# Weight sums kept within the SSD half, and transposes emitted one weight tile later

## The chip, the cores and the metric

The kernel runs on one core of a Trainium2 chip. The core has a matrix engine (TensorE, PE in the profile, with its weight loads shown as PEld), a vector engine (VectorE, DVE), a scalar engine (ScalarE, ACT), GpSimd (POOL) and a queue engine (SyncE, SP). Each takes its instructions in order. SP and POOL issue the transfers here. The metric is device time in microseconds; the median of three runs of the kernel before is 900.42 us (898.77 to 902.17).

## What is computed

Two layers over a sequence of 512 tokens and 1024 channels, in float32: a bidirectional SSD mixer, then a bidirectional gated linear attention (GLA), each with a residual, and a norm at the end. Cut to what matters:

```
def ssd_mixer(u, ...):
    z, xbc, dt = jnp.split(u @ w_in, [D_INNER, D_INNER + SSD_CONV_DIM], axis=-1)
    xbc = jax.nn.silu(dwconv(xbc, conv_w, conv_b)).astype(f32)
    xh, bm, cm = jnp.split(xbc, ...)
    y = (ssd_scan(xh, dt[:, :, 0], a[0], bm, cm)
         + rev(ssd_scan(rev(xh), rev(dt[:, :, 1]), a[1], rev(bm), rev(cm)))
         + xh * d_skip.astype(f32)[:, None])
    y = y.reshape(bsz, seq, D_INNER) * jax.nn.silu(z.astype(f32))
    y = rmsnorm(y.reshape(bsz, seq, SSD_GROUPS, ...), gnorm.reshape(SSD_GROUPS, -1))
    return y.reshape(bsz, seq, D_INNER).astype(u.dtype) @ w_out

def gla_mixer(u, ...):
    q, k, v, z, gl = jnp.split(u @ w_in, ...)
    ...
    o = gla_scan(q, k, v, lg[:, :, 0]) + rev(gla_scan(rev(q), rev(k), rev(v), rev(lg[:, :, 1])))
    o = rmsnorm(o, onorm).reshape(bsz, seq, D_INNER) * jax.nn.silu(z.astype(f32))
    return o.astype(u.dtype) @ w_out
...
h = h + ssd_mixer(rmsnorm(h, ssd_norm[0]), ...)
h = h + gla_mixer(rmsnorm(h, gla_norm[0]), ...)
return rmsnorm(h, final_norm)
```

## The kernel before

**Matmuls and weight tiles.** Every large product is made of three passes (`mm3`, lines 149 to 151): both operands are split into a high part `whi`, `uh` and a rest `wlo`, `ul`, and the product of the two rests is left out. The weights come through one list of tiles of 512 KB (`Weights`). A tile is loaded by SP into one of three `wraw` buffers (line 68), split by ScalarE (line 88 or 93) and VectorE (line 89 or 94), and used by 24 matmuls of 512 columns (12 in the block products of the GLA half). `W.next()` hands out the tile at place `W.pos`; it first emits the splits up to two tiles ahead and then calls whatever stands in `W.beside` for this place. The SSD half has the tiles 0 to 64, counted from 0; the GLA half begins with tile 65.

**The SSD half.** Eight groups g. For each, `proj_group` computes B, C and two tiles of x (matmuls `pch`), with a convolution on VectorE (line 530) and a tanh on ScalarE (line 534); every second group begins with four tiles for z (`ptk`). The scan of group g - 1 (`scan_group`, a generator) is emitted in steps between the tiles of group g. Its steps: transposes of x and B (`ptx` line 590, `ptb` line 595), copied out by ScalarE (`xt`, `bt`); the product `cb`; the decay weights of four chunks (`weights`: ScalarE lines 653 and 661, VectorE lines 658 and 662) on `bct`; the states (`pts`); then for each half of the sequence `outputs` (matmuls `pti` lines 677 and 679, `pyi` line 694, VectorE lines 700 to 704, squares on ScalarE line 708, the root on GpSimd lines 317 and 318, scaling on ScalarE line 711, giving `y`) and `transposed` (four transposes `pty` line 719, split into `yh`, `yl`, which the output projection `po` reads). `bct` is a broadcast of 1 MB, one for each group and half, loaded by SP (line 575) into three buffers, so the load for a half waits until the `pyi` of three halves earlier have read theirs. The last output projection (`pr`) and the second norm (`ptn`) end the half.

**The GLA half.** Four heads. v and z of a head come from seven block products (`pb`) in place of eight, and these need four sums of weight blocks, `w1` to `w4`, of 1 MB each. They are made in DRAM by transfers that GpSimd issues (`Blocks.step`, eight to a head, 32 in all: a copy at line 274, or an accumulating transfer at line 272), in the list of the program named `wsumw`. Each is paced: `add_manual_dep` makes it wait for the last split emitted so far. After the block products come the scores (`bd` line 1010, `pta` lines 1018 and 1019), the output projection of the head before (`po`), q and k of the next, and the outputs (`pto`, `ptyg`).

**What sets the order.** A scheduler orders each engine's instructions by priority, beginning from the order in which the code emits them. `tc.high_priority(offset=-100)` puts the transposes of `trans` 100 places behind. The places of the sums are a table of tile numbers:

```
n1 = last1 + 1
at = [8 + (n1 - 10) * i // 26 for i in range(26)] + [n1 + i for i in (20, 26, 32, 37, 42, 47)]
```

## Time and profile before

| | us |
|---|---|
| median of three runs | 900.42 (898.77 to 902.17) |
| profiled execution | 896.58 |
| its span, first to last instruction | 894.9 |
| TensorE busy | 845.0 |
| VectorE busy | 680.5 |
| ScalarE busy | 510.7 |
| GpSimd busy | 95.6 |

The rows that follow below are from this one profiled execution. Times are in microseconds from the start of the span. Matmuls overlap each other, so TensorE's busy share is not its share of peak; what counts is where it stands still and for whom. A row of the timeline gives start, duration, engine, line, operation, output<-inputs, shapes, how many instructions are merged, and in brackets the idle time of the engine before it with the engine that ended it.

### The profile page before, as it was taken

The numbers are of one execution on the slowest core, as the hardware profiler recorded it, in microseconds if no ns is written. First come the engines' busy times: TensorE is split into PE (matmuls) and PEld (weight loads), VectorE is DVE, ScalarE is ACT, GpSimd is POOL, SyncE is SP. The second block draws the span as 40 slices with busy tenths as digits, with TensorE's granted clock in tenths as the row PEclk, the third lists the DMA queues.
The fourth block names the chain that finished last, engine by engine and source line by source line (L and its number), as shares of the span: only waits on it lengthen the run. The fifth ranks groups of instructions, "written<-read, shape, count | busy, mean of one in ns | idle before, by whom it ended". The sixth has DMA issues, their size and how long they took to land.

```text
span 894.9 us, 11286 instructions
## 1 busy us (share of the span) xinstructions
PE 845.0 (94%) x3976; PEld 688.2 (77%) x3976; DVE 680.5 (76%) x1044; ACT 510.7 (57%) x1078; POOL 95.6 (11%) x156
## 2 busy tenths in 40 slices
PE   7999999999999999998799999989999989999996
PEld 5778778788888788887677777868787878778875
DVE  5499889897678986779696799877946785588644
ACT  5338698746575466654665466674527542665333
POOL 3001011101011001010102510020002000110012
PEclk9999999999999999999999999999999999999999
DMA  6447578555867575864350236428643763245202
GB/s 227 120 133 273 142 190 228 157 155 190 165 184 216 131 246 118 225 167 127 108 197 24 65 110 203 120 49 215 207 118 73 216 190 87 71 151 179 71 1 94
DMA packets 90198, 132.92 MB, mean 149 GB/s; under 512 B 7969, under 2 KB 49149, under 8 KB 87966
## 3 DMA queue, kind: packets, MB, share of 16 engines
q1 hardware_dynamic: 78716, 97.46, 34.6%
q0 software_dynamic: 11424, 34.74, 17.2%
q8 instruction: 31, 0.51, 0.2%
q14 instruction: 25, 0.20, 0.1%
q10 hardware_dynamic: 2, 0.00, 0.0%
HBM read 129.96 MB, written 35.78 MB: 185 GB/s over the span
## 4 chain that ended last, share of the span: by engine, by line
PE 60%; DVE 14%; DMA 9%; ACT 8%; issue 5%; POOL 3%; POOLq 0%; SPq 0%; ACTq 0%; DVEq 0%
DMA bct<-cumd 5%; PE pch L150 5%; PE pch L149 5%; PE pch L151 4%; PE po L150 4%; PE po L151 4%; PE po L149 4%; PE pb L149 3%; PE pb L151 3%; PE pb L150 3%; PE pyi L694 3%; PE ptk L149 3%; PE ptk L151 3%; PE ptk L150 3%; DVE wlo L89 2%
## 5 line engine op out<-in xcount | busy, mean ns | idle before, releaser
L89 DVE TENSOR_TENSOR wlo<-wraw,whi 128x1024 fp32r<-128x1024 f32 (+1 forms) x114 | 140.4, 1234 | 76.8 <-ACT whi L88 76.1
L88 ACT CAST whi<-wraw 128x1024 fp32r<-128x1024 f32 (+1 forms) x114 | 118.9, 1043 | 137.1 <-PE pch L150 40.6
L150 PE MATMUL pch<-ul,whi 128*128 128x512 f32 (+2 forms) x336 | 133.4, 397 | 0.0
L151 PE MATMUL pch<-uh,wlo 128*128 128x512 f32 (+2 forms) x336 | 132.7, 395 | 0.6 <-DVE wlo L89 0.5
L149 PE MATMUL pch<-uh,whi 128*128 128x512 f32 (+2 forms) x336 | 132.9, 396 | 0.0
L151 PEld LDWEIGHTS pch<-uh,wlo 128*128 128x128 f32 (+2 forms) x336 | 62.5, 186 | 15.0 <-DVE wlo L89 1.5
L149 PEld LDWEIGHTS pch<-uh,whi 128*128 128x128 f32 (+2 forms) x336 | 62.5, 186 | 13.8
L150 PEld LDWEIGHTS pch<-ul,whi 128*128 128x128 f32 (+2 forms) x336 | 62.5, 186 | 13.7 <-issue 0.3
L530 DVE SCALAR_TENSOR_TENSOR cv<-pch,colA,cv 128x511 f32<-128x511 f32 (+1 forms) x96 | 70.9, 743 | 0.7
L93 ACT ACTIVATE whi<-wraw,colB 128x512 fp32r<-128x512 f32 x58 | 38.8, 716 | 37.7 <-PE pch L150 17.3
L653 ACT ACTIVATE bct<-bct,eb 128x128 f32<-128x128 f32 x128 | 41.4, 391 | 22.2 <-DMA bct<-cumd 22.2
L149 PE MATMUL ptk<-whi,uh 128*128 128x512 f32 x128 | 52.3, 409 | 1.2 <-DVE cv L530 1.2
L151 PE MATMUL ptk<-whi,ul 128*128 128x512 f32 x128 | 51.3, 402 | 0.0
L150 PE MATMUL ptk<-wlo,uh 128*128 128x512 f32 x128 | 51.2, 401 | 0.0
L317 POOL TENSOR_SCALAR rs<-ss 128x2 f32<-128x2 f32 (+1 forms) x32 | 10.0, 312 | 369.5 <-ACT gy L1066 238.8
L94 DVE SCALAR_TENSOR_TENSOR wlo<-wraw,colB,whi 128x512 fp32r<-128x512 f32 x58 | 41.7, 747 | 10.1 <-ACT whi L93 9.8
L661 ACT ACTIVATE bct<-bct,eb 128x128 f32<-128x128 f32 x128 | 41.3, 392 | 13.3 <-DVE bct L658 13.3
L149 PE MATMUL pb<-whi,uh 128*128 128x512 f32 x96 | 38.5, 401 | 2.0 <-DVE u L866 2.0
L151 PE MATMUL pb<-whi,ul 128*128 128x512 f32 x96 | 38.6, 402 | 0.0
L150 PE MATMUL po<-wlo,yh 128*128 128x512 f32 x96 | 38.5, 401 | 0.0
L150 PE MATMUL pb<-wlo,uh 128*128 128x512 f32 x96 | 38.3, 399 | 0.0
L149 PE MATMUL po<-whi,gyh 128*128 128x512 f32 x96 | 37.9, 395 | 0.0
(307 smaller groups left out, 2037.5 us busy)
## 6 DMA issues: line engine op xcount, KB each, us to landing
wraw<-in_ssd_w_in_dram SPq DMA_DIRECT2D x48, 512.0 KB, 5.3
wsumw<-in_gla_w_in_dram POOLq DMA_DIRECT2D x24, 1024.0 KB, 9.9
bct<-cumd SPq DMA_DIRECT2D x16, 1024.0 KB, 4.9
wraw<-in_gla_w_in_dram SPq DMA_DIRECT2D x32, 512.0 KB, 3.9
wraw<-wsumw SPq DMA_DIRECT2D x32, 512.0 KB, 3.6
wraw<-in_ssd_w_out_dram SPq DMA_DIRECT2D x16, 512.0 KB, 4.6
wraw<-in_gla_w_out_dram SPq DMA_DIRECT2D x16, 512.0 KB, 3.7
h<-in_x_dram SPq DMA_DIRECT2D x4, 512.0 KB, 6.5
```

The source lines that it names most:

```text
L88: self.mark = nc.scalar.copy(vh, raw)
L89: nc.vector.tensor_tensor(out=vl, in0=raw, in1=vh.bitcast(F32), op=ALU.subtract)
L93: self.mark = nc.scalar.mul(hs[j], raw[:, j], g)
L94: nc.vector.scalar_tensor_tensor(out=ls[j], in0=raw[:, j], scalar=g, in1=hs[j].bitcast(F32), op0=ALU.mult, op1=ALU.subtract)
L149: nc.tensor.matmul(pt, lhsT=a[0], rhs=b[0], start=first, stop=False)
L150: nc.tensor.matmul(pt, lhsT=a[0], rhs=b[1], start=False, stop=False)
L151: nc.tensor.matmul(pt, lhsT=a[1], rhs=b[0], start=False, stop=last)
L317: nc.gpsimd.tensor_scalar(out=dst, in0=ss, scalar1=mul, scalar2=add, op0=ALU.mult, op1=ALU.add)
L530: nc.vector.scalar_tensor_tensor(out=cv[:, o0:o1], in0=pt[:, o0 + s : o1 + s], scalar=cwt(j, a), in1=cv[:, o0:o1], op0=ALU.mult, op1=ALU.add,)
L653: nc.scalar.activation(bct[:, r], bct[:, r], AF.Identity, bias=TM["eb"][:, cc, i : i + 1])
L661: nc.scalar.activation(et[:, r], et[:, r], AF.Exp, bias=TM["eb"][:, cc, i : i + 1])
L694: nc.tensor.matmul(py[:, q * 256 + r * 64 : q * 256 + (r + 1) * 64], lhsT=et[:, r], rhs=xt[:, cc, r * 64 : (r + 1) * 64], start=True, stop ...
```

## The change

Three edits. The sums: all 32 stand now at tiles 8 to 57 (`8 + 51 * i // 32`); before, 26 stood at tiles 8 to 60 and six in the GLA half. The transposes: `trans` no longer emits them at once with a low priority, but enters them in `W.beside`, one place ahead, so that they are emitted when the tile after the next is taken, and `tc.issue_after(W.mm.ins)` holds them on TensorE behind the last matmul emitted by then. In the generator the outputs of the second half are thereby emitted ahead of the transposes of the first. The buffers: `y` has three in place of two. `W.beside` holds lists now.

```
-        self.beside.get(i, lambda: None)()
+        for f in self.beside.pop(i, ()):
+            f()
...
-            nc.tensor.matmul(pt, lhsT=a[1], rhs=b[0], start=False, stop=last)
+            W.mm = nc.tensor.matmul(pt, lhsT=a[1], rhs=b[0], start=False, stop=last)
...
-        n1 = last1 + 1
-        at = [8 + (n1 - 10) * i // 26 for i in range(26)] + [n1 + i for i in (20, 26, 32, 37, 42, 47)]
+        at = [8 + 51 * i // 32 for i in range(32)]
         for i, pos in enumerate(at):
-            W.beside[pos] = lambda b=blocks[i // 8], n=i % 8: b.step(n)
+            W.beside.setdefault(pos, []).append(lambda b=blocks[i // 8], n=i % 8: b.step(n))
...
-                    return sp.tile([64, L], F32, tag=n, name="d" + n, bufs=4 if n == "st" else 2)
+                    return sp.tile([64, L], F32, tag=n, name="d" + n, bufs={"st": 4, "y": 3}.get(n, 2))
...
-                    y = sp.tile([P, 2, 256], F32, tag="y", name="y", bufs=2)
+                    y = sp.tile([P, 2, 256], F32, tag="y", name="y", bufs=3)
...
                 def trans(half):
-                    with tc.high_priority(offset=-TRANS_BEHIND):
-                        transposed(half)
+
+                    def f():
+                        with tc.issue_after(W.mm.ins):
+                            transposed(half)
+
+                    W.beside.setdefault(W.pos + 1, []).append(f)
```

Lines behind 122 of the changed kernel have numbers higher by 1 to 4 (the third pass of `mm3` is line 152, `pty` line 720, the sums lines 273 and 275).

GpSimd's queue at the end of the sums, before (in the GLA half; `rs` is the root of a norm, `wsumw_3_106` to `_109` are w1, w2, w3, w4 of head 3, in the order 106, 107, 108, 109):

```order
L318 TENSOR_TENSOR rs<-rs,nhalf 128x1
L272 DMA wsumw_3_106<-in_gla_w_in_dram 512x512
L317 TENSOR_SCALAR rs<-ss 128x1
L318 TENSOR_TENSOR rs<-rs,nhalf 128x1
L272 DMA wsumw_3_108<-in_gla_w_in_dram 512x512
L274 DMA wsumw_3_107<-wsumw_3_106 16x16384
L272 DMA wsumw_3_107<-in_gla_w_in_dram 512x512
```

The same queue now, at the end of the SSD half (two columns in `rs` for the SSD norms):

```order
L275 DMA wsumw_3_107<-wsumw_3_106 16x16384
L317 TENSOR_SCALAR rs<-ss 128x2
L318 TENSOR_TENSOR rs<-rs,nhalf 128x2
L273 DMA wsumw_3_107<-in_gla_w_in_dram 512x512
L275 DMA wsumw_3_109<-wsumw_3_107 16x16384
L273 DMA wsumw_3_109<-in_gla_w_in_dram 512x512
L317 TENSOR_SCALAR rs<-ss 128x2
```

The sums of head 3 stood between the roots of the GLA norms, and now stand between those of the SSD groups, the last three with no root between them.

TensorE in the scan of group 3, before, 36.7 tiles into the program (`pch` are matmuls of the weight tile; numbers in names are buffers):

```order
L150 MATMUL pch<-ul,whi_2328 128x512
L719 MATMUL pty<-idn,y 128x128
L677 MATMUL pti<-st_2139,cv_1624 128x256
L679 MATMUL pti<-st_2134,cv_1624 128x256
L694 MATMUL pyi<-xt_2041,bct 128x64 x8
L677 MATMUL pti<-st_2145,cv_1624 128x256
L151 MATMUL pch<-uh,wlo_2329 128x512
L719 MATMUL pty<-idn,y 128x128
```

Now, 35.0 tiles into the program:

```order
L152 MATMUL pch<-uh,wlo_2235 128x512
L677 MATMUL pti<-st_2143,cv_1626 128x256
L679 MATMUL pti<-st_2138,cv_1626 128x256
L694 MATMUL pyi<-xt_2037,bct 128x64 x4
L677 MATMUL pti<-st_2149,cv_1626 128x256
L694 MATMUL pyi<-xt_2037,bct 128x64 x4
L150 MATMUL pch<-uh,whi_2284 128x512
```

The second half's `pti` and `pyi` stood behind the first transpose of the first half; they now stand 1.7 tiles earlier, and the four transposes follow nine matmuls later in one piece.

ScalarE around the decay weights that follow there, before (`whi_2495` is the split of tile 39, `cv` a convolution's first term):

```order
L88 CAST whi_2495<-wraw_2493 128x1024
L526 ACTIVATE cv_2477<-pch,colB,colA 128x512
L653 ACTIVATE bct<-bct,eb 128x128 x3
L708 ACTIVATE xc,ss<-y 128x256 x2
L653 ACTIVATE bct<-bct,eb 128x128 x2
L711 ACTIVATE y<-y,rs 128x256 x2
```

And now (`whi_2452` is the split of tile 38):

```order
L88 CAST whi_2452<-wraw_2450 128x1024
L526 ACTIVATE cv_2441<-pch,colB,colA 128x512
L653 ACTIVATE bct<-bct,eb 128x128 x6
L708 ACTIVATE xc,ss<-y 128x256 x2
L653 ACTIVATE bct<-bct,eb 128x128 x2
L711 ACTIVATE y<-y,rs 128x256 x2
L88 CAST whi_2493<-wraw_2491 128x1024
```

The first `bct` instructions moved ahead by one weight tile, together with the squares and the scaling of y behind them.

## Rows read from the trace of the kernel before

**Rows 1.** The page, part 1: busy us (share) xinstructions by engine.

```profile
PE 845.0 (94%) x3976; PEld 688.2 (77%) x3976; DVE 680.5 (76%) x1044; ACT 510.7 (57%) x1078; POOL 95.6 (11%) x156
```

**Rows 2.** TensorE's waits, 55 to 500 us: waiter <- releaser: total, times, longest.

```profile
PE pty L719 <- ACT y L711: 8.6, 5, 4.1
PE ptb L595 <- ACT xt L591: 4.9, 3, 2.2
PE ptx L590 <- DVE cv L535: 2.1, 2, 1.1
```

**Rows 3.** The waits of all engines, 55 to 500 us: ScalarE for `bct`.

```profile
ACT bct L653 <- DMA bct<-cumd: 22.2, 7, 7.9
```

**Rows 4.** Timeline of ScalarE, where it waits for `bct`.

```profile
166.64 2.16 ACT L653 ACTIVATE bct<-bct,eb 128x128 f32<-128x128 f32 x7 [3.20 <-DMA bct<-cumd]
...
396.02 1.28 ACT L653 ACTIVATE bct<-bct,eb 128x128 f32<-128x128 f32 x4 [4.67 <-DMA bct<-cumd]
...
430.45 0.69 ACT L653 ACTIVATE bct<-bct,eb 128x128 f32<-128x128 f32 x2 [3.56 <-DMA bct<-cumd]
```

**Rows 5.** Timeline of TensorE, 402 to 408 us, transposes of x and B.

```profile
402.98 0.98 PE L590 MATMUL ptx<-idn,cv 128*128 128x128 f32 x7 [1.14 <-DVE cv L535]
...
407.44 0.66 PE L595 MATMUL ptb<-idn,cv 128*128 128x128 f32 x4 [2.21 <-ACT xt L591]
```

**Rows 6.** Timeline of TensorE, the first transpose of group 6.

```profile
433.61 0.33 PE L719 MATMUL pty<-idn,y 128*128 128x128 f32 x1 [4.07 <-ACT y L711]
```

**Rows 7.** Timeline of TensorE, first `bd` and last group of `pta` in heads 1 to 3.

```profile
623.17 0.61 PE L1010 MATMUL bd<-sc,sc 128*128 128x128 f32 x4
...
643.66 0.46 PE L1018 MATMUL pta<-sc,sc 128*128 128x128 f32 x2 [1.18 <-DVE al L155]
...
716.34 0.61 PE L1010 MATMUL bd<-sc,sc 128*128 128x128 f32 x4
...
738.69 0.46 PE L1018 MATMUL pta<-sc,sc 128*128 128x128 f32 x2 [2.92 <-DVE al L155]
...
811.38 0.61 PE L1010 MATMUL bd<-sc,sc 128*128 128x128 f32 x4
...
830.12 0.40 PE L1018 MATMUL pta<-sc,sc 128*128 128x128 f32 x2
```

**Rows 8.** The chain of waits: start, us, what (a DMA from issue to landing).

```profile
421.55 8.88 DMA bct<-cumd
...
610.18 0.23 PE pb L151
...
716.16 10.31 DMA wraw<-in_gla_w_out_dram
```

**Rows 9.** Timeline of GpSimd: two of the weight sums it issues.

```profile
417.53 1.07 POOL L272 DMA_DIRECT2D wsumw<-in_gla_w_in_dram  x1 [15.58 <-ACT whi L93]
...
712.54 1.03 POOL L272 DMA_DIRECT2D wsumw<-in_gla_w_in_dram  x1 [13.57 <-ACT whi L88]
```

**Rows 10.** A 20 us stretch: length, busy PE, PEld, DVE, ACT, POOL, PEclk, DMA, GB/s.

```profile
420.00:440.00 20.00, 15.93 (x83) 13.65 (x82) 12.09 (x21) 9.05 (x28) 0.90 (x2) 0.91 0.56 156
```

**Rows 11.** The tiles `bct`, then `wsumw` on GpSimd: time from issue to landing.

```profile
DMA to landing us min/median/max: 4.7/4.9/8.9
...
DMA to landing us min/median/max: 5.3/8.6/13.6
```

**Rows 12.** Timeline, the last `pyi` and the scaling of y: group 6, then 7.

```profile
435.42 2.77 PE L694 MATMUL pyi<-xt,bct 128*128 128x64 f32 x16
...
446.91 0.91 ACT L711 ACTIVATE y<-y,rs 128x256 f32<-128x256 f32 x2 [0.33 <-POOL rs L318]
...
475.93 1.00 PE L694 MATMUL pyi<-xt,bct 128*128 128x64 f32 x8
...
481.79 0.91 ACT L711 ACTIVATE y<-y,rs 128x256 f32<-128x256 f32 x2 [0.47 <-POOL rs L318]
```

## The prediction, made before the changed kernel was run

> **What bounds the kernel now.** I read the engines' shares first: TensorE is busy 94% of the 894.9 us span, every other engine less [rows 1]. So a gain can only come out of TensorE's remaining gaps, and the question is which gaps this change reaches. Second, the list of what TensorE itself waits for in the SSD half (55 to 500 us). Three waits lead it: `pty`, the transposes of the gated outputs, for y from ScalarE (8.6 us in 5 waits); `ptb`, the transposes of B, for ScalarE's copy of `xt` (4.9 us in 3); `ptx`, the transposes of x, for VectorE's convolution (2.1 us in 2) [rows 2]. Third, ScalarE's own waits in that half: the one that matters is for the landing of `bct`, the 1 MB broadcast of cumulative decays, 22.2 us in 7 waits [rows 3]. ScalarE works in order, so while it waits for `bct` nothing behind it moves. The rows show it: ScalarE stands 3.20 us for the `bct` of group 3 and 4.67 us for that of group 7 (group 5's wait is shorter), and 3.56 us in the last pass [rows 4]; the TensorE stalls follow some 10 us behind the third (ptx 1.14, ptb 2.21) [rows 5] and at once behind the last (pty 4.07) [rows 6].
>
> In the GLA half I compare the same stretch of three heads, from the first `bd` matmul to the last group of `pta` matmuls: 623.17 to 643.66, 716.34 to 738.69, 811.38 to 830.12, that is 20.49, 22.35 and 18.74 us [rows 7]. The work is the same. The first two hold a wait for VectorE of 1.18 and 2.92 us, the third none. In the second, a weight load issued at 716.16 took 10.31 us [rows 8], and beside it stands a weight sum that GpSimd issued at 712.54 [rows 9]; it was the last of the sums, so the third head meets none.
>
> **Part 1: six sums leave the GLA half.** Of the 32 sums, six were issued after 500 us. With them gone I expect heads 1 and 2 to take the time of head 3: (20.49 - 18.74) + (22.35 - 18.74) = 5.4 us. The rest of TensorE's order in that half is unchanged, and the two waits alone are 1.18 + 2.92 = 4.1 us, so the lower bound is 4.1. I take **-5.4**. No reader comes too early: the six are sums for head 3, and they now end within the SSD half.
>
> **Part 2: the second half's outputs move ahead of the first half's transposes.** Before, TensorE came to the `pyi` matmuls of a group's second half behind `pty` of its first (group 3: 36.71 tiles into the program). Now they stand at 35.00, and `pty` nine matmuls later; the third `y` buffer is what lets both halves live at once. One tile is 24 matmuls at 0.23 us [rows 8], 5.5 us. The third of three `bct` buffers comes free with those `pyi`, so the `bct` load for the first half of the group after next starts 1.7 tiles earlier, while ScalarE's first use of it moves forward by one tile only (it stood behind the split of tile 39 and now behind that of 38). The load gains 0.7 tile = 3.9 us of lead. Against ScalarE's waits of 3.20 and 4.67 us this leaves 0 and 0.8 [rows 4]. The waits of ptb and ptx behind them sum to 4.9 + 2.1 = 7.0 us [rows 2]. A released ScalarE may show VectorE as next in line, since its own order barely changes and it is the second busiest engine, so I take **-6.5**, with bounds 0 and -7.0.
>
> **Part 3: the last stretch.** The 4.07 us stall at 433.61 comes from a `bct` load issued at 421.55 that took 8.88 us [rows 6, 8]. Its buffer comes free at the same tile as before, so it isn't issued earlier. Two things change. ScalarE's squares of y now stand ahead of the `bct` instructions (before, two of these stood in front). And the sum issued at 417.53 beside the load [rows 9] falls away: sums now stand at tiles 55 and 57, the first of them a plain copy, the second paced by the split of tile 59, after the load's start. At a free landing of 4.9 us [rows 11] it lands at 426.5, and y would be delayed by under 1 us. Around the stall the granted clock is down too, 0.91 of the full 2.4 GHz in the stretch 420 to 440, in which TensorE was busy for 15.93 us [rows 10]: 9% of that is 1.4 us. Bounds 0 and -5.5 (4.07 + 1.4); I take **-2.5**.
>
> **Part 4: the pinned transposes.** A pinned transpose costs nothing while y is ready when TensorE comes to it. Between the last pyi and y the trace has 5.8 us in the emptiest place, the second half of group 7 (475.93 + 1.00 to 481.79 + 0.91), and 9.6 us in the crowded pass of group 6 (435.42 + 2.77 to 446.91 + 0.91) [rows 12]. Most places have cover of 30 matmuls or more (6.9 us and the small matmuls between). Four are short: group 0 and group 7, second half, 18 matmuls (4.1 us); group 7, first half, 23 matmuls with about 2.6 us of small work; group 6, second half, 24 matmuls with 1.7 us. At 5.8 us these cost 2 x 1.7 = 3.4; at 9.6 us, 2 x 5.5 + 1.7 + 2.4 = 15. Today's pty waits other than the 4.07 sum to 8.6 - 4.1 = 4.5 [rows 2]. The balance lies between -1 and +10.5; the free value is nearer because the last group's ScalarE is nearly free of scan work, so **+1.5**.
>
> **Part 5: a denser SSD half.** All 32 sums are now issued between tiles 8 and 57, one in 1.6 tiles where it was one in 2.1. A sum takes 8.6 us to land [rows 11]; 26 of them fill 224 us of the 404 between 61 and 465 us (55%), and 32 fill 275 of some 370 (74%). So one load in five more meets a sum. A `bct` load takes 4.9 us free and 8.9 met [rows 11]; over 13 loads that is 13 x 0.19 x 4.0 = 10 us of landing, of which only what exceeds the new lead of Part 2 counts. I take **+1**, bounds 0 and the price of the second rival. On GpSimd's queue the sums now end ahead of the y scalings they could hold up: a sum that reads the sum before it (tile 54 to 55, one tile apart) waits for that landing, but the next `rs` pair stands two sums later and belongs to a y that is not made until tile 57. SP's queue keeps its loads, with a `bct` moved ahead of a weight load in five places; the weight loads run two tiles ahead, which covers it.
>
> **Sum.** -5.4 - 6.5 - 2.5 + 1.5 + 1.0 = -11.9 us. The profiled execution took 896.58 us around its span of 894.9, which gives 884.7. That execution was 3.8 us below the median of the runs, 900.42; against the median the forecast is **888.5 us**.
>
> **Rivals.** *The pins bite.* TensorE then stands at the four short places, and at no other, for the slow 9.6 us: the +10.5 of Part 4 in place of +1.5. 900.42 - 11.9 + 9.0 = 897.5 us, no change by what a measurement can tell (0.5%, 4.5 us). For it speaks that TensorE waited at three of those places already; against it, that the crowded 9.6 us has the `bct` wait in it.
>
> *The loads starve (slower).* Place: the `bct` loads that ScalarE waits for. If each of the seven waits of rows 3 grows by the 4.0 us of a met load, ScalarE waits 28 us longer. Of 22.2 us waited today 7.0 + 4.1 = 11.1 reached TensorE, a half, so TensorE loses 14 us, and Parts 2 and 3 bring nothing: 900.42 - 5.4 + 14 = 909 us. It decides against the change once the `bct` waits on ScalarE exceed 22.2 + 2 x 5.4 = 33 us. For it: at 421.55 the trace has exactly this, a sum in flight and 8.88 us. Against it: the median of all 16 landings is 4.9 us although sums were in flight over half the time [rows 11], and the earlier release. The Trainium skill (DMA: Bandwidth & Descriptors, section Queues, rings and completion order) says that each DMA engine alternates between the queues that have work, packet by packet, so by an estimate from it a met load runs at half rate, 9.8 us for 4.9, and the rival's extra would be 7 x 4.9 / 2 = 17 us in place of 14; the row's 8.88 agrees with it for a load that was met for most of its way.
>
> *Only the GLA half gains.* VectorE, the second busiest, takes over the SSD half's gaps as soon as ScalarE is freed, and Parts 2 to 5 sum to zero: 900.42 - 5.4 = 895.0 us. For it: VectorE stood ahead of ptx at 402.98 [rows 5]; against it: over the whole span VectorE is busy 76% [rows 1].
>
> **How the numbers follow.** Forecast 0.63, only GLA 0.12, pins bite 0.13, loads starve 0.12. Faster by over 0.5% (below 895.9) takes the forecast and most of the GLA-only case: 0.72. Within 0.5%: the pins and what is left of it, 0.16. Slower: 0.12. With every part at its good end (-5.4 - 7.0 - 5.5 - 1) the time is 881.5; I set the low end at 880. At the high end 902 takes in the pins and half of Part 5's price, and leaves out the starved case.
>
> **What would show it.** Right: heads 1 and 2 at 18.7 us from `bd` to `pta`; no ScalarE wait for `bct` over 1 us in the passes of groups 3, 5 and 7, and no ptb wait over 1 us; the pty wait of group 6's first half under 2 us. Wrong: `bct` landings with a median above 6 us, or pty waits that sum to more than 8.6 us. What I can least bound is that the scheduler has re-ordered VectorE and ScalarE in the SSD half throughout, and small gaps could open in places that the trace of before doesn't have.

## The result, and the profile after

| | before | changed |
|---|---|---|
| median of four runs, us | 901.29 (898.77 to 903.03) | 889.93 (887.70 to 890.59) |
| ratio, 95% interval | | 0.9872 (0.9840 to 0.9903) |
| profiled execution, us | 896.58 | 890.59 |
| its span, us | 894.9 | 888.9 |

The changed kernel is 1.3% faster: 11.4 us by the medians, against 11.9 forecast. In the four later groups of runs the median of the kernel before was 898.1 to 899.2 us, and against those the gain is 8 to 9 us. The two profiled executions are only 6.0 us apart, since the one of before is faster than all four timed runs of its kernel and the one of after is the slowest of its four. The traces account for these 6.0 us; the other 5.4 us lie in the spread between executions and are seen in no trace here. Of all runs below one is left out, an execution of `tiny_sums` that took 2164.9 us where its other four took 871.5 to 872.6.

The engines' shares hardly move (busy us, share, instructions), and TensorE leads as in [rows 1]:

```profile
PE 846.9 (95%) x3976; PEld 692.4 (78%) x3976; DVE 678.5 (76%) x1044; ACT 508.8 (57%) x1078; POOL 95.3 (11%) x156
```

**The GLA half** did what was forecast. The timeline of TensorE, first `bd` and last `pta` group of heads 1 to 3, to set beside [rows 7]:

```profile
622.54 0.61 PE L1014 MATMUL bd<-sc,sc 128*128 128x128 f32 x4
...
641.27 0.40 PE L1022 MATMUL pta<-sc,sc 128*128 128x128 f32 x2
...
713.89 0.60 PE L1014 MATMUL bd<-sc,sc 128*128 128x128 f32 x4
...
732.62 0.40 PE L1022 MATMUL pta<-sc,sc 128*128 128x128 f32 x2
...
805.25 0.61 PE L1014 MATMUL bd<-sc,sc 128*128 128x128 f32 x4
...
823.98 0.40 PE L1022 MATMUL pta<-sc,sc 128*128 128x128 f32 x2
```

All three stretches are 18.73 us from start to start, with no wait in the last group. Before, the first two took 20.49 and 22.35.

**The SSD half** is where it becomes interesting. TensorE's waits there (55 to 500 us: total, times, longest), then ScalarE's for `bct`, to set beside [rows 2, 3] (`pty` is line 719 in both kernels, not 720 in the changed one as said above):

```profile
PE ptx L590 <- DVE cv L535: 8.1, 2, 6.1
PE pty L719 <- ACT y L711: 3.1, 2, 2.7
...
ACT bct L653 <- DMA bct<-cumd: 20.8, 5, 8.0
```

The `ptb` waits are gone, and `pty` for ScalarE's y fell from 8.6 to 3.1 us. But there is a new wait of 6.1 us ahead of `ptx`, and ScalarE waits for `bct` nearly as long as before (20.8 against 22.2 us).

Every matmul of `mm3` is in both traces, so the time from the first matmul of one weight tile to the first of another can be compared between kernels. I use such stretches all through this text; for three of them the windows (length, busy PE, granted clock, DMA share, GB/s), first of before and then of after:

```profile
389.65:424.40 34.75, 30.98 (x156) 1.00 0.51 146
424.40:466.68 42.28, 36.09 (x182) 0.96 0.45 145
466.68:499.98 33.30, 29.75 (x152) 1.00 0.15 47
```

```profile
391.66:431.08 39.42, 33.24 (x159) 0.91 0.50 137
431.08:466.74 35.66, 35.09 (x190) 1.00 0.48 132
466.74:496.50 29.76, 27.85 (x139) 1.00 0.10 23
```

These are tiles 53 to 57, 57 to 61 and 61 to 65. The first lost 4.7 us, the second won 6.6 and the third 3.5. Over tiles 9 to 65 the balance is -4.0 us, and the GLA half's -5.5 is partly taken back by 2.8 us of matmuls at a lower granted clock in two stretches, 539.48 to 560.26 us (the last block products of head 0) and 587.24 to 611.66 us.

The lost 4.7 us can be followed from engine to engine. Lines of the timeline, of GpSimd, SP, ScalarE, VectorE and TensorE:

```profile
378.96 1.02 POOL L273 DMA_DIRECT2D wsumw<-in_gla_w_in_dram  x1 [9.50 <-ACT whi L88]
387.54 0.53 POOL L275 DMA_DIRECT2D wsumw<-wsumw  x1 [7.57 <-ACT whi L88]
...
379.86 0.37 SPq L68 DMA_DIRECT2D wraw<-in_ssd_w_in_dram  x1
380.39 0.46 SPq L575 DMA_DIRECT2D bct<-cumd  x1
...
394.91 1.87 ACT L653 ACTIVATE bct<-bct,eb 128x128 f32<-128x128 f32 x6 [6.99 <-DMA bct<-cumd]
...
397.90 0.73 DVE L658 COPY_PREDICATED bct<-mlt,bct 128x512 f32<-128x512 uint8 x1 [7.35 <-ACT bct L653]
...
403.40 0.66 PE L590 MATMUL ptx<-idn,cv 128*128 128x128 f32 x2 [6.14 <-DVE cv L535]
```

Read it from the bottom. TensorE waits 6.14 us for a convolution; VectorE had stood 7.35 us for ScalarE; ScalarE stood 6.99 us for the `bct` of group 7, which SP had issued at 380.39. The wait ends 14.5 us after the issue. Beside it two sums were under way (issued at 378.96 and 387.54) and a weight tile of 0.5 MB ahead of it on the same queue. And the stretch has a mean clock of 0.91: within the stall and behind it, from 400.3 to 407.1 us, the granted clock is at 1.2 GHz, the lower of its two levels. So the load is issued earlier than before, as forecast, and comes hardly sooner. Is that the sums, or the new order? The median landing of `bct` rose too, from the 4.9 us of [rows 11]:

```profile
DMA to landing us min/median/max: 4.7/6.6/9.3
```

Such a line must be read with care. The longest landing in it is 9.3 us, though the load of group 7 took 14.5: the profile gives a landing to only 9 of the 16 loads here, and to 7 of 16 in the kernel before, and in both the load that ScalarE stands for in group 7 is not among them. From the semaphore updates in the traces all 16 can be worked out: their median is 6.1 us before and 7.1 after.

### The profile page after: what moved, and what is told of

It reads as the page before. It is cut to its first block, busy times and chain, and to the rows that moved or that the text cites. A ratio compares the mean times of both kernels' runs of the same rounds, so it can differ in the third digit from the quotient of the medians.

```text
span 888.9 us, 11282 instructions
## 1 busy us (share of the span) xinstructions
PE 846.9 (95%) x3976; PEld 692.4 (78%) x3976; DVE 678.5 (76%) x1044; ACT 508.8 (57%) x1078; POOL 95.3 (11%) x156
## 3 DMA queue, kind: packets, MB, share of 16 engines
q1 hardware_dynamic: 78716, 97.46, 35.6%
## 4 chain that ended last, share of the span: by engine, by line
PE 70%; DVE 10%; ACT 9%; issue 4%; DMA 3%; POOL 3%; POOLq 0%; SPq 0%; ACTq 0%; DVEq 0%
PE po L150 5%; PE po L151 5%; PE po L152 5%; PE pch L151 5%; PE pch L150 5%; PE pch L152 5%; PE pb L150 4%; PE pb L152 4%; PE pb L151 4%; PE ptk L150 3%; PE ptk L151 3%; PE ptk L152 3%; PE pyi L694 3%; DMA bct<-cumd 3%; DVE wlo L89 2%
## 5 line engine op out<-in xcount | busy, mean ns | idle before, releaser
L317 POOL TENSOR_SCALAR rs<-ss 128x2 f32<-128x2 f32 (+1 forms) x32 | 11.8, 369 | 433.9 <-ACT gy L1070 323.6
L653 ACT ACTIVATE bct<-bct,eb 128x128 f32<-128x128 f32 x128 | 41.4, 393 | 21.0 <-DMA bct<-cumd 20.8
L692 ACT ACTIVATE xc<-xt,coef 128x64 f32<-128x64 f32 x128 | 33.7, 337 | 10.8 <-DVE coef L614 10.7
L151 PE MATMUL pb<-wlo,uh 128*128 128x512 f32 x96 | 39.4, 411 | 0.0
L152 PE MATMUL pb<-whi,ul 128*128 128x512 f32 x96 | 39.4, 410 | 0.0
L389 DVE TENSOR_TENSOR h<-h,po 128x512 f32<-128x512 f32 x48 | 32.0, 683 | 9.0 <-PE po L152 9.0
```

The source lines that it names most:

```text
L151: nc.tensor.matmul(pt, lhsT=a[0], rhs=b[1], start=False, stop=False)
L152: W.mm = nc.tensor.matmul(pt, lhsT=a[1], rhs=b[0], start=False, stop=last)
L389: nc.vector.tensor_tensor(out=hs, in0=hs, in1=pts[t], op=ALU.add)
L653: nc.scalar.activation(bct[:, r], bct[:, r], AF.Identity, bias=TM["eb"][:, cc, i : i + 1])
L692: nc.scalar.mul(xc[:, q, k], xt[:, cc, k], coef[:, cc, r : r + 1])
```

## The experiments

The kernels were run in groups, each with runs of the kernel before (median 901.29 us in the group of the changed kernel, 898.1 to 899.2 in the others), so the ratios carry over from group to group better than the medians. The last column is the time from TensorE's first weight tile matmul of the program to that of tile 65 in the profiled execution, so the whole SSD half.

| kernel | median us | ratio to before (95%) | SSD half us |
|---|---|---|---|
| before | | 1 | 489.4 |
| changed | 889.93 | 0.9872 (0.9840 to 0.9903) | 485.4 |
| `sums_only` | 896.60 | 0.9972 (0.9953 to 0.9992) | 495.1 |
| `trans_only` | 893.06 | 0.9940 (0.9916 to 0.9964) | 484.4 |
| `before_no_sums` | 876.28 | 0.9751 (0.9728 to 0.9774) | 474.4 |
| `after_no_sums` | 871.13 | 0.9699 (0.9675 to 0.9723) | 470.0 |
| `last5_moved` | 883.00 | 0.9829 (0.9790 to 0.9868) | 480.3 |
| `sums_apart` | 879.76 | 0.9790 (0.9757 to 0.9823) | 478.6 |
| `sums_apart2` | 872.72 | 0.9695 (0.9670 to 0.9719) | 470.9 |
| `last5_back` | 880.60 | 0.9802 (0.9765 to 0.9840) | 478.3 |
| `trans_at_once` | 898.28 | 0.9984 (0.9962 to 1.0005) | 493.9 |
| `two_y` | 889.76 | 0.9901 (0.9872 to 0.9929) | 487.6 |
| `tiny_sums` | 871.90 | 0.9687 (0.9664 to 0.9711) | |
| `tiny_sums_b` | 873.50 | 0.9723 (0.9661 to 0.9785) | 471.7 |

### The two halves of the change, with and without sums

`sums_only` keeps the new table and undoes the rest; `trans_only` undoes the table:

```diff
-            def f():
-                with tc.issue_after(W.mm.ins):
-                    transposed(half)
-            W.beside.setdefault(W.pos + 1, []).append(f)
+            with tc.high_priority(offset=-TRANS_BEHIND):
+                transposed(half)
...
-y = sp.tile([P, 2, 256], F32, tag="y", name="y", bufs=3)
+y = sp.tile([P, 2, 256], F32, tag="y", name="y", bufs=2)
```

```diff
-at = [8 + 51 * i // 32 for i in range(32)]
+n1 = last1 + 1
+at = [8 + (n1 - 10) * i // 26 for i in range(26)] + [n1 + i for i in (20, 26, 32, 37, 42, 47)]
```

> The new places of the 32 sums, with the transposes and the two y buffers of the kernel before. Theory (a bct load that meets a sum lands late; the later transposes give the lead that hides part of it): the GLA half gains its 5.5 us, the SSD half loses 2 to 5 us because six more sums meet the loads and nothing frees the buffers sooner; 0 to 3.5 us faster than the kernel before, ScalarE waits over 25 us for bct. Rival (crowding costs nothing, the 6 us stall ahead of ptx in the pass of group 7 is made by the new order of the transposes): the SSD half is unchanged, 5.5 us faster than before, no ptx wait above 3 us.

> The later, pinned transposes and three y buffers, with the sums at their places of before (26 in the SSD half, 6 in the GLA half). Theory (crowding): the GLA half is unchanged, heads 1 and 2 at 20.5 and 22.4 us from bd to pta; the SSD half gains 5 to 9 us because the freed buffers let the bct loads start sooner and fewer sums meet them; 892 to 896 us on a kernel before of 901, and no ptx wait of 6 us. Rival (the new order of the transposes makes the stall): the ptx wait of about 6 us in the pass of group 7 is there also here, and the SSD half gains no more than the 3.5 us of the changed kernel: 897 to 898 us.

In the two kernels without sums the loop that issues them is left out, and the GLA half loads input blocks in their place:

```diff
-for src in (self.b11, self.b21, w["w2"], w["w1"], w["w3"], w["w4"], self.b22)[a:b]:
+for src in (self.b11, self.b21, self.b12, self.b22, self.b12, self.b21, self.b22)[a:b]:
...
-for i, pos in enumerate(at):
-    W.beside.setdefault(pos, []).append(lambda b=blocks[i // 8], n=i % 8: b.step(n))
```

> The changed kernel with the 32 sums left out; the GLA half loads blocks of its input weights of the same size in place of the sums, so its matmuls and transfers stay the same and the output is not the reference's. Theory (crowding): bct loads land in a median of 4.9 us or less, ScalarE waits under 8 us for them, the 6.3 us stall ahead of ptx goes, and the whole is 4 to 8 us faster than the changed kernel: 882 to 886 us. Rival (order of the transposes): the stall stays, 889 to 890 us.

> The kernel before with the 32 sums left out in the same way, its output again not the reference's. Theory: the GLA half gains the 5.5 us of the six sums, and the SSD half 2 to 5 us, since the buffers still come free late but no load takes 8.9 us: 890 to 893 us. Against the changed kernel without sums the difference is the worth of the later transposes alone: 5 to 9 us. Rival (sums in the SSD half cost nothing): 895.5 us, and the worth of the transposes without sums is the 3.5 us that the changed kernel shows.

**Measured.** `sums_only`: the GLA stretches gain their 5.5 us, the SSD half loses 5.7; 2.5 us faster in all by the ratio, as the theory has it, though ScalarE waits only 17.4 us for the landing of `bct` (its waits of 12.8 us for VectorE stand behind). No `ptx` wait above 3 us: the rival is right in that alone. `trans_only`: heads 1 and 2 of the GLA half keep their waits, the SSD half gains 5.0 us, and the stall of 6 us in group 7 is not there, so the new order of the transposes does not make it. It has a `ptx` wait of 2.9 us in an earlier pass. In the traces `trans_only` has the same order on every engine as the changed kernel, but for the sums; `sums_only` differs from the kernel before in 27 of TensorE's 3976 instructions too, so its 5.7 us need not be the sums' alone.

The surprise is the size in the kernels without sums. I expected 4 to 8 us from the sums and found 15.6 by the ratios (0.9872 to 0.9699) and 18.8 by the medians; in the traces it is 18.3 us, of which 15.4 in the SSD half. For the kernel before it is 22 us by the ratio and 21.4 in the traces, of which 6.5 in the GLA half and 15.0 in the SSD half. The sums had been costing the SSD half 15 us all along, and the rival, that they cost nothing there, falls. The later transposes are worth 5.2 us without sums (876.28 - 871.13), 5.4 us with the old table (0.9940), and about 9 us with the new one by the ratios (0.9872 against 0.9972; 6.7 by the medians, 9.7 in the SSD half of the traces). So the two parts of the change don't look independent: the six sums more cost the SSD half 5.7 us with the old transposes and 1.0 us with the new, by one trace of each.

### Is it the meeting with one load?

`last5_moved` takes the last five sums away from that one load and leaves the order on every other engine as it is:

```diff
-at = [8 + 51 * i // 32 for i in range(32)]
+at = [8 + 51 * i // 32 for i in range(27)] + [53, 54, 55, 58, 59]
```

> The changed kernel with the last five sums (places 51, 52, 54, 55, 57) at 53, 54, 55, 58 and 59, so that none is in flight beside the bct load of group 7 that took 14.5 us; every other engine's order is unchanged. Theory (a sum in flight slows the load, and the late load makes the stall): that load lands in 5 to 6 us, the wait of 6.3 us ahead of ptx goes, weight tiles 53 to 57 take 32 to 33 us in place of 39.4, nothing else moves: 883 to 885 us on a kernel before of 900. Rival (the crowding moves with the sums: whatever they meet next waits as long): the same 889 us, with a new stall of some 6 us between tiles 55 and 65.

**Measured.** 883.0 us. Tiles 53 to 57 take 32.25 us in place of 39.43, and the stall of 6 us is gone. Tiles 57 to 61 give back 1.1 us of it. Tiles 41 to 49, where nothing was moved, take 1.6 us longer than in the changed kernel's trace, which shows how far two executions can differ. The theory holds, in place and size.

`sums_apart` does the same for all 32, and `sums_apart2` corrects six of its places (its expectation says five). In the traces both keep the changed kernel's order on every engine, but for the sums:

```diff
-at = [8 + 51 * i // 32 for i in range(32)]
+at = [8, 8, 11, 12, 15, 20, 22, 23, 24, 24, 28, 29, 31, 33, 34, 36,
+      37, 37, 38, 39, 41, 44, 45, 46, 47, 47, 49, 53, 54, 55, 58, 59]
```

```diff
-at = [8, 8, 11, 12, 15, 20, 22, 23, 24, 24, 28, 29, 31, 33, 34, 36,
-      37, 37, 38, 39, 41, 44, 45, 46, 47, 47, 49, 53, 54, 55, 58, 59]
+at = [5, 6, 11, 12, 15, 20, 22, 23, 24, 24, 28, 29, 31, 32, 33, 36,
+      37, 37, 38, 39, 41, 44, 45, 46, 47, 47, 49, 53, 54, 55, 57, 60]
```

> The changed kernel with all 32 sums at places (8 8 11 12 15 20 22 23 24 24 28 29 31 33 34 36 37 37 38 39 41 44 45 46 47 47 49 53 54 55 58 59) chosen so that by the landings of the changed kernel's trace hardly one is in flight beside a bct load. Theory: of the 15.4 us that the sums cost the SSD half (485.4 against 470.0 us to weight tile 65) 8 to 13 come back, and the sum of ScalarE's waits for bct falls below 13 us: 875 to 882 us. Rival (what the sums cost is not the meeting with bct but their traffic beside all loads, the weights' too): no more than the stall of group 7 comes back, 883 to 889 us.

> The kernel sums_apart with five places changed: the first two sums at 5 and 6 in place of 8 and 8, those at 33 and 34 at 32 and 33, the last two at 57 and 60 in place of 58 and 59. Theory (meeting of a bct load): the 2.0 us stall ahead of ptx at 84.6, the 2.2 us one at 280.3 and the 1.5 us one at 451.1 go, since no sum is in flight beside the loads of 70 to 77, of 264 and of 421; some 5 us below sums_apart, 873 to 876 us on a kernel before of 899. Rival (other loads pay): the first nine tiles, which load the input and the first weights, get 2 to 5 us longer, and the kernel stays at 878 to 882 us.

**Measured.** `sums_apart` comes to 879.8 us, in the slower half of what I expected, with ScalarE's waits at 16.0 us where I had said below 13. Its trace shows why. Issues of SP in the pass of group 5, first of `sums_apart` and then of `sums_apart2` (start, us):

```profile
263.77 3.88 SPq L575 DMA_DIRECT2D bct<-cumd  x1
```

```profile
261.15 0.45 SPq L575 DMA_DIRECT2D bct<-cumd  x1
```

A sum issued at 261.74 stood right ahead of the first, and the issue of the load by itself took 3.88 us in place of 0.45. With that sum one tile earlier the issue is short, and the `ptx` wait of 2.1 us behind it goes, as do a `ptx` wait of 1.8 us that ended at 86.81 and a `pti` wait of 1.3 us that ended at 452.79. `sums_apart2` takes 872.7 us, a little below what I expected: 16 us less than the changed kernel by the ratios (0.9695 against 0.9872), and the same as the kernel that issues no sums at all (0.9699). Its SSD half is 470.9 us against 470.0. The first tiles don't get longer (56.5 us to tile 9, as in the changed kernel), so the rival falls.

What moved is TensorE's waiting, not the amount transferred. ScalarE's wait for `bct` in `sums_apart2`, then the landings of `bct`:

```profile
ACT bct L653 <- DMA bct<-cumd: 9.2, 2, 8.2
...
DMA to landing us min/median/max: 4.7/5.9/8.6
```

The kernel without sums has 9.8 us in 4 waits, the longest 8.1: the long one is there without any sum, and TensorE does not feel it. Two `bct` loads of `sums_apart2` still have a sum beside them and take 8.6 and 9.3 us (issued at 241.72 and 353.46); nobody waits for them. The median landing of 5.9 us is nearer to the changed kernel's 6.6 than to the 4.8 without sums (9 of 16 loads each; of all 16, the medians are 6.2, 7.1 and 5.9). `sums_apart`, 7 us slower, has 5.0. So it is not how often a load is met that counts but whether ScalarE is about to need it.

`last5_back` is the reverse of the first test, made in the fast kernel:

```diff
-47, 47, 49, 53, 54, 55, 57, 60]
+47, 47, 49, 51, 52, 54, 55, 57]
```

> The kernel sums_apart2 with its last five sums put back to the places of the changed kernel (51, 52, 54, 55, 57). Theory (meeting of the sums with one bct load): the stall of some 6 us ahead of ptx in the pass of group 7 comes back alone, weight tiles 53 to 57 take 39 to 40 us in place of 32.25, all other stretches of the SSD half stay within 0.5 us: 879 to 881 us on a kernel before of 899. Rival (the loss in group 7 needs the sums that stood earlier in the changed kernel too, through lateness that adds up): under 3 us of it comes back, 873 to 876 us.

**Measured.** 880.6 us, as the theory has it. Tiles 53 to 57 take 39.85 us in place of 32.25, and every other stretch of the SSD half from tile 9 on is within 0.3 us of `sums_apart2`. The load, the sums beside it, ScalarE's first use and the window of tiles 53 to 57 (length, busy PE, granted clock, DMA share, GB/s) in the two kernels, first `sums_apart2`, then `last5_back`:

```profile
372.90 0.44 SPq L575 DMA_DIRECT2D bct<-cumd  x1
...
386.93 1.08 POOL L273 DMA_DIRECT2D wsumw<-in_gla_w_in_dram  x1 [2.34 <-ACT whi L88]
...
380.33 1.86 ACT L653 ACTIVATE bct<-bct,eb 128x128 f32<-128x128 f32 x6
...
384.17:416.42 32.25, 31.73 (x159) 1.00 0.74 180
```

```profile
372.46 0.46 SPq L575 DMA_DIRECT2D bct<-cumd  x1
...
371.07 1.02 POOL L273 DMA_DIRECT2D wsumw<-in_gla_w_in_dram  x1 [9.62 <-ACT whi L88]
379.63 0.53 POOL L275 DMA_DIRECT2D wsumw<-wsumw  x1 [7.54 <-ACT whi L88]
...
386.83 1.87 ACT L653 ACTIVATE bct<-bct,eb 128x128 f32<-128x128 f32 x6 [6.83 <-DMA bct<-cumd]
...
383.73:423.58 39.85, 33.84 (x160) 0.91 0.47 137
```

Without a sum beside it the load is there within 7.4 us (372.90 to 380.33, no wait; by its semaphore it landed at 378.99); with the two it takes 14.4. The windows show the other part of the price: busy PE is 33.84 us for the work that took 31.73, at a granted clock of 0.91. Of the 7.6 us lost, 2.1 are slower matmuls behind the stall.

Where the load loses its time can be read from the single transfer packets in the traces, and it is not in its own movement. Its 128 packets of 8 KB take 3.3 us in `sums_apart2` and 3.4 in `last5_back`. But on SP's queue they come behind the weight tile issued just before, whose 1024 packets are of 512 B. In `last5_back` that tile shares the DMA engines with the first sum, whose packets are of 2 KB, and from 375 to 379 us it moves only 79 to 82 packets in each us, where it reaches 559 in `sums_apart2`; so `bct` begins at 380.54, 8.1 us after its issue in place of 2.4. The Trainium skill (DMA: Bandwidth & Descriptors, section Queues, rings and completion order) has each DMA engine take packets in turn from the queues that have work. The trace agrees: in the same four us the sum moves 80 to 83 packets in each. The packets are unequal, so the tile keeps far less than half of its rate. The second sum, a copy from one sum to the next in 16 packets of 64 KB and 2.4 us each, then delays the end. The landing is reported in sixteen parts; the last of `bct`'s own packets ends at 383.90, thirteen parts are in by then, and the other three come at 386.33 to 386.80, when the copy's packets have ended. The changed kernel has the same picture: the tile ahead lands at 389.38, the data of `bct` have moved by 391.98, and the last of the sixteen parts comes at 394.88. That the copy's packets hold these last parts is read from the times alone; neither sum was moved without the other.

### Traffic or GpSimd's queue?

A sum does more than move bytes: it stands in GpSimd's queue, which also makes the roots `rs` of the gated norm. `tiny_sums` keeps all 32 in the queue, with their waits, and takes the bytes away:

```diff
+dst, src = dst[0:4], src[0:4]
 if add:
     dma = nc.gpsimd.dma_start(dst, src, accum_op=ALU.add)
```

> The changed kernel with each of the 32 sums cut to 4 of its 512 rows (8 KB in place of 1 MB), at the same places, with the same waits for the pace on GpSimd's queue; the GLA half loads blocks of its input weights of the same size, and the output is not the reference's. Theory A (what the sums cost is their traffic beside the loads): the traffic is gone, so nearly all of the 15 to 19 us between the changed kernel and the one without sums comes back: 871 to 874 us. Rival B (GpSimd's queue: a sum that waits for its pace, or is being issued, holds the small rs operations of the gated norm behind it, as ahead of the pty wait of 2.9 us at 126.2): that wait stays, together with others of its kind, and the kernel takes 876 us or more. Both can hold in part: each us above 871 is the queue's.

> The same kernel as tiny_sums, for a profile that can be read (the one taken was of an execution of 2163 us). Theory A (traffic): no pty wait of 2.9 us near 126 us, SSD half within 1.5 us of the kernel without sums (470.0 us to weight tile 65). Rival B (GpSimd's queue holds rs behind a sum that waits for its pace): the pty wait of 2 to 3 us in that place is still there, and weight tiles 13 to 17 take 38 us or more in place of 35.55.

**Measured.** 871.9 us, and 873.5 in the two runs of `tiny_sums_b`, against 871.1 without any sum; by the ratios 0.9687 and 0.9723 against 0.9699. So the queue by itself costs between nothing and some 2 us, and the traffic nearly all the rest. The trace of `tiny_sums_b` has 471.7 us in the SSD half, 1.7 above the kernel without sums and a little over the 1.5 that Theory A allowed, and 36.0 us in tiles 13 to 17, where the changed kernel takes 39.4 and the one without sums 35.6. There the two causes act together. GpSimd and ScalarE in the changed kernel, then in `tiny_sums_b`:

```profile
126.16 1.05 POOL L273 DMA_DIRECT2D wsumw<-in_gla_w_in_dram  x1 [5.64 <-ACT whi L88]
126.85 1.08 POOL L317 TENSOR_SCALAR rs<-ss 128x2 f32<-128x2 f32 x1
...
128.77 0.91 ACT L711 ACTIVATE y<-y,rs 128x256 f32<-128x256 f32 x2 [2.95 <-POOL rs L318]
```

```profile
122.49 0.82 POOL L274 DMA_DIRECT2D wsumw<-in_gla_w_in_dram  x1 [3.85 <-ACT whi L88]
123.09 0.67 POOL L318 TENSOR_SCALAR rs<-ss 128x2 f32<-128x2 f32 x1
...
124.60 0.91 ACT L712 ACTIVATE y<-y,rs 128x256 f32<-128x256 f32 x2 [0.66 <-POOL rs L319]
```

In both, `rs` stands behind a sum. In the first it costs ScalarE 2.95 us and then TensorE a `pty` wait of 2.72; in the second 0.66 us, and the `pty` wait is 0.43, as without sums (0.39). The sum adds onto the result of the copy issued just ahead of it, so it cannot go before that has landed, and a copy of full size needs 5.5 us or more. The trace of the changed kernel shows that this landing, and not the split that the profile names, ended the wait: the queue's wait for it lasts until 125.53, the copy of 119.92 landed at 125.50, and the split had ended at 124.08.

### What of the transposes does the work?

Built without `issue_after`, the changed kernel gives the same program, instruction for instruction and wait for wait on every engine, so there was nothing to run. The pin does nothing; what works is the emission one tile later. `trans_at_once` takes the delay away and `two_y` the third buffer:

```diff
-            W.beside.setdefault(W.pos + 1, []).append(f)
+            transposed(half)
```

```diff
-y = sp.tile([P, 2, 256], F32, tag="y", name="y", bufs=3)
+y = sp.tile([P, 2, 256], F32, tag="y", name="y", bufs=2)
```

> The changed kernel with the transposes emitted in their own step at normal priority, one weight tile earlier than in the changed kernel (three y buffers and the new places of the sums kept). Theory (the delay of a tile is what keeps TensorE from waiting for y): TensorE meets the transposes before ScalarE has scaled y, pty waits sum to 10 us or more in the SSD half, 893 to 900 us. Rival (any early order does, since it is the low priority of before that cost the time): pty waits under 6 us, 887 to 891 us.

> The changed kernel with two y buffers as before; the order on every engine is that of the changed kernel. Theory: the third buffer is what lets the second half's first y operation run before the first half's transposes have been read; without it VectorE waits for the transposes in 8 passes, 0.3 to 1 us each, in part hidden: 1 to 5 us slower than the changed kernel, 891 to 895 us. Rival (the transposes are done by then in any case): the same, 889 to 890 us.

**Measured.** `trans_at_once` gives the whole gain back: 898.3 us, and TensorE's waits for y (55 to 500 us) are

```profile
PE pty L719 <- ACT y L711: 16.2, 13, 4.4
```

as the theory has it. `two_y` misses its theory: the order on the engines is the same with two buffers, TensorE's waits nearly so (`pty` 3.1 us, `ptx` 7.7), and its median is that of the changed kernel. By the ratios, 0.9901 against 0.9872 with overlapping intervals, it would be 2.6 us slower, and its SSD half is 2.2 us longer in the trace, while the span is 0.6 shorter; so a small worth of the buffer can't be excluded, and the rival fits better.

## Why the prediction was right, and where not

The total was right within half a microsecond by the medians of the first runs. Against the 898.1 to 899.2 us of the kernel before in the later groups the gain is 8 to 9 us, and then the forecast promised some 3 us too much. The terms were not all right.

**Part 1** (-5.4): right. Heads 1 and 2 fell to 18.73 us, 5.4 us by these rows, and in every kernel with the new table.

**Part 2** (-6.5): the place was right, the size not. The earlier release came, the wait of group 3 went, and `trans_only` shows the whole worth of the later transposes as 5.4 us (3.2 to 7.5). But one step failed: "The load gains 0.7 tile = 3.9 us of lead. Against ScalarE's waits of 3.20 and 4.67 us this leaves 0 and 0.8." That held the landing fixed while the load was moved in time, and the sums with it. The lead itself came nearly as forecast: ScalarE was ready for the load of group 7 4.2 us after its issue before and 7.5 us after it now. But at its new time this load met two sums and took 14.5 us where it had taken 8.8. The lead was eaten in that one place, 6.99 us of wait where 0.8 was left. The third `y` buffer, which this part called what lets both halves live at once, is not needed for it.

**Part 3** (-2.5, bounds 0 and -5.5): the right mechanism, too small, and outside its own bound. Tiles 57 to 61 gained 6.6 us. That it is the sum that fell away, as the part said, and not the transposes, is shown by three kernels: the stretch takes 36.2 us in `sums_only` and 35.6 in `before_no_sums`, but 40.5 in `trans_only`, against 42.3 before. Most of the 6.6 us are the stall of [rows 6], 4.07 us, faster matmuls at the full clock where [rows 10] had 0.91 (busy PE 36.09 to 35.09 us), and a second `pty` wait, 1.65 us before and 0.57 after, which the part left out. I had taken less than half of the first two.

**Part 4** (+1.5, -1 to +10.5): the wrong sign. The late transposes do not cost, they gain: tiles 61 to 65 went from 33.3 us to 29.8 or 30.0 in every kernel that emits them a tile later, whatever the sums do, and only to 32.4 in the two without them (`sums_only`, `before_no_sums`). Of the four short covers three were long enough, with waits of at most 0.6 us. At the fourth, group 0's second half, TensorE waited 2.72 us (129.34), but for a y that the late `rs` on GpSimd held up; without sums 0.39 us are left there. That the transposes had stood too early there is what remains as an explanation; `trans_at_once`, with 31.8 us, speaks for it.

**Part 5** (+1): under-sized. With the new transposes the new table costs +1.0 us in the SSD half (485.4 against 484.4), but this is a balance: the 4.8 us that it gains in tiles 57 to 61 against `trans_only` must be set against 5.8 us that it loses elsewhere. Those 5.8 us are what Part 5 should have held.

So the sum runs: -5.4, about -5 for the transposes in place of -5.0 (Parts 2 and 4 together), and +1.0 in place of -1.5 (Parts 3 and 5 together): only the last pair is off, by 2.5 us. Against that stand 2.8 us lost in the traces to the clock in the GLA half, which no part had, and the spread named at the beginning, which brings the first medians back to the forecast; that much of the agreement is luck.

**The rivals.** "The loads starve" was the right mechanism in one place: a load met by sums, ScalarE behind it, TensorE behind that. Its point of decision, 33 us of `bct` waits on ScalarE, was not reached (20.8), since the meeting mattered for one load and not for seven. What the prediction did not see is that this rival had been paid already: 15 us of the SSD half before. The argument against it, that the median of all 16 landings was 4.9 us with sums in flight over half the time, is the error. That median is of the 7 loads to which the profile gives a landing; of all 16 it is 6.1 us, and the loads of groups 3 and 7, for which ScalarE stood 3.20 and 4.67 us, took 7.6 and 8.8 and are not among the 7. And the loads that count are in any case the few that ScalarE stands for. Nor does the 8.88 us of 421.55 show a load at half rate: its own packets took 3.5 us there, and the rest of the time lies ahead of them, while the weight tile in front moved beside the sum. "The pins bite" falls with Part 4, and "only the GLA half gains" with tiles 57 to 65.

**The signs named beforehand.** Heads at 18.7 us: yes. No `bct` wait above 1 us in groups 3, 5 and 7: yes for 3, no by a little for 5 (1.23 us at 276.05), no for 7. No `ptb` wait: yes. The `pty` wait of group 6's first half under 2 us: yes, none is left. The sign against, a median `bct` landing above 6 us, came true as well (6.6), and rightly: it pointed to the 16 us that `sums_apart2` then found. But as a sign it is a poor one, as the 5.9 us of that kernel and the 5.0 us of the slower `sums_apart` show.

## What to carry to other kernels

Background transfers that can go anywhere within a long stretch are not free there, and not evenly dear: list the loads that an engine actually stands for, and place the transfers between them. Here 32 transfers of 1 MB cost the SSD half 15 us spread evenly, and about 1 us once they were placed by the trace. Look also at what stands ahead of such a load on its own queue: here the weight tile in front lost more time to the sums than the load itself. Before trusting a median landing time, look how many of the loads it covers, and at the landing of the load behind each wait; and when a change moves a load in time, look up what is in flight at its new time.

## What the runs showed of the hardware that I had not expected

- The issue of a load on SP can itself be held up: 0.34 to 0.46 us as a rule for `bct`, but 3.88 us two us behind a sum's issue (`sums_apart`, 263.77), and up to 2.6 us in the changed kernel. A late load can thus be late before it begins. In the traces every issue of a load in the SSD half that took over 1.5 us stands 0.7 to 4.3 us behind a copy from one sum to another, the kind with packets of 64 KB; behind the same copy cut to 8 KB it took 0.34 us (`tiny_sums_b`, 135.60).
- A copy sum takes from 5.5 us when alone; two issued together took 7.8 and 11.7 us (`sums_apart`, 186.61 and 187.26).
- The granted clock falls with a stall of some 6 us and costs 2 us on top: in the changed kernel it is at 1.2 GHz from 400.3 to 407.1 us, and the mean over the stretch is 0.91 of 2.4 GHz. And it can fall behind a wait of only 2.0 us: the changed kernel has it at 1.2 GHz from 547.1 to 550.5 us, and the stretch from 539.48 to 560.26 us takes 20.8 us where the kernel before, with the same wait, takes 19.2 at full clock. TensorE's first matmul behind the wait, after and before, then the stretch behind it after (length, busy PE, granted clock, DMA share, GB/s):

```profile
547.08 0.77 PE L150 MATMUL pb<-whi,uh 128*128 128x512 f32 x1 [2.00 <-DVE u L870]
```

```profile
550.55 0.47 PE L149 MATMUL pb<-whi,uh 128*128 128x512 f32 x1 [2.04 <-DVE u L866]
```

```profile
547.10:550.50 3.40, 3.40 (x8) 0.50 0.60 162
```

All kernels with the later transposes but `sums_apart2` have this fall, and `trans_at_once` too; the wait is 1.95 to 2.05 us in all thirteen traces. I did not settle what decides it.
